# Gate-row offsets and a column copy moved to ScalarE, head selectors made one head ahead, and other reorderings in a hybrid mLSTM/GLA block on Trainium2

## The chip, the cores and the metric

The kernel runs on one core of a Trainium2 chip. The core has a matrix engine (TensorE, PE in the profile), a vector engine (VectorE, DVE), an activation engine (ScalarE, ACT), a general engine (GpSimd, POOL) and SyncE (SP), whose queue issues most DMAs. Each engine runs its own instructions strictly in the order in which the program gave them, and waits by semaphore for what another engine must finish first. The metric is the device time of one execution, in microseconds.

## The reference

One decoder block on 512 positions plus 16 learned meta tokens (padded to 9 chunks of 64), model width 1024, float32. Cut to what matters:

```python
xn = rmsnorm(h, norm1_g)
proj = xn @ w_in                   # split into mq,mk,mv,mi,mf,mo,gq,gk,gv,ga,gr,gate_m,gate_g
mq, mk = split(silu(causal_conv4([mq, mk])))
logi, logf = mi + b_i, log_sigmoid(mf + b_f)            # 4 heads
hm = mlstm_chunkwise(mq * 128**-0.5, mk, mv, logi, logf) # stabilised by a running maximum m_t
hm = head_rmsnorm(hm) * sigmoid(mo)
loga = log_sigmoid(ga @ g_a2 + g_a2_b) / 16
hg = head_rmsnorm(gla_chunked(gq * 128**-0.5, gk, gv, loga)) * silu(gr)
merged = sigmoid(gate_m) * (hm @ w_branch_m) + sigmoid(gate_g) * (hg @ w_branch_g)
h = h + merged @ w_out
ff = silu(hn @ w_ff_gate) * (hn @ w_ff_up)   # hn = rmsnorm(h, norm2_g)
out = rmsnorm(h + ff @ w_ff_down, final_g)
```

Per mLSTM head, position j takes from source s the weight exp(bc_j - bc_s + logi_s - m_j) times q.k; `gate_rows` in the kernel prepares these exponents as rows, and shifts them by each 128-column chunk's distance.

## The kernel before, in words

**Products.** Every weight matrix is streamed as units of 128 x 1024 (tile `raw`, loaded by SP; some parts are added by GpSimd DMAs). A unit is split in two fp32r tiles: ScalarE casts it to `whi` (L190), VectorE takes the difference into `wlo` (L195). Each 128x128 block then costs three matmuls: high by high, high by low, low by high. Plain units run through `mm3` (L304 to L306), 512 or twice 264 columns at a time.

Part of the units come in pairs, done by a Strassen-Winograd scheme: instead of eight half products seven are made, named p7, q1, p3, q6, p4, p2, q5, each four blocks deep and 256 or 272 columns wide (`seven`, L346 to L348). A pair has three PSUM banks: `bx` collects q1, then q6 (with the former p3 pending) and q5; `bz` collects p7 and p4; `by` p2. Between products, banks are copied out while the sum goes on: s1 (ScalarE copy of `bx`) and s7 (of `bz`) when p3 begins, that is, right ahead of q6, which writes on in `bx`; then s2, s5 and others. p3 of a pair is left pending and done in the next pair, at p3's place. Three pairs have no p3 pending when they begin: the first of the merge gates (`gm`, gate_m of the reference), the first of the GLA queries (`gq`) and the first of the feed-forward part. There nothing stands between the first two products and q6. The first merge-gate pair is the first pair of the program.

**Order.** The schedule is written by hand; nothing reorders it. `unit` and `pair` call, after block k of a product, what is due there: the copies of the banks and the split steps for a coming unit (tables `PLAIN`, `FIRST`, `SECOND`, which name the product and block after which each step is issued). Then `tick()` advances the side work by one step: generators that end a step with `yield n`, n being the ticks until the next. `mixers` holds the mLSTM and GLA heads, of which one runs at a time; the others (`side`) run next to each other. So a `yield 6` moves all later steps of that head, and of the heads behind it, six ticks down.

**The steps that the change names.** `gate_rows` builds, on 32 partitions, forget-gate sums `bl`, input exponents `a0` and their running maximum `ml` (whose input `d0` is zeroed first, L658); then ten offset rows (L685), each `bl`'s value at a chunk's end added to 128 columns of a row; TensorE transposes them (L701) into one bank that is copied out as `acol` (L695), and `gts.ready` lets the heads begin. `mlstm` (L877 on) starts a head: a selector (`sel`, cast by ScalarE, L883) picks the head's rows of `gts.R` by two matmuls (L886, L887) into the banks `pb` and `pm`; ScalarE copies `pb` into `nml` (L890), VectorE adds the mask to it (L891), ScalarE takes the exponential of `pm` (`em`). Then come the scores k.q (L908 to L910), the exponentials with `acol` as bias, and their products `wh`, `wl` (L919, L928). Their sum over sources is cast and split (L936, L941) and multiplied with ones (L955). `head_out` normalises a head (L802 to L839), with a Ln, an Exp and so two loads of an activation table. `conv`, `gates_of` and the evacuations of projections (L595, L617) take banks from the same eight. `mixed_x` copies activations for the pairs (L582, L546). `final` (L1487 on) is the last norm.

Of the kernel before, what the change touches and what calls it, by code (L numbers as in the profile page):

```python
# [9 lines left out]
F32R = mybir.dt.float32r  # L10
I32 = mybir.dt.int32
AF = mybir.ActivationFunctionType
ALU = mybir.AluOpType
PSUM = bass.MemoryType.PSUM

P = 128
D = 1024
KT = 8
NM = 16
NS = 512  # L20
NT = NM + NS
HALF = NT // 2
H = 4
DFF = 2816
FT = DFF // P
EPS = 1e-6
TAU = 16.0
QS2 = 128.0
CH = 128
# [73 lines left out]
def hybrid_block(ctx: ExitStack, tc: tile.TileContext, xT, wst, par, con, out):  # L103
# [5 lines left out]
    def nm(s):  # L109
        cnt[0] += 1  # L110
        return f"{s}_{cnt[0]}"
# [6 lines left out]
    def tt(dt=F32, n=NT, p=P):  # L118
        t = tpool.tile([P, TW], dt, tag="t", name=nm("t"))
        return t[:p, :n]  # L120
# [7 lines left out]
    def act(o, i, func, **kw):  # L128
        want = TABLE.get(func)
        if want is not None and table[0] not in want:  # L130
            table[0] = want[0]
            if func != AF.Silu:
                S.preload_act_table_set(want[0])
        S.activation(o, i, func, **kw)  # L134
# [122 lines left out]
    def g_lo(u):  # L257
# [6 lines left out]

    PLAIN = {"s": [(split_hi, 2), (split_lo, 4)], "e": [(e_hi, 1), (e_lo, 3), (s2, 4)],
             "a": [(a_hi, 1), (a_lo, 3), (f_hi, 4), (s4, 5)]}
    FIRST = {"s": [(split_hi, ("q1", 2)), (split_lo, ("p3", 1))],
             "e": [(e_hi, ("q1", 2)), (e_lo, ("p3", 1)), (s2, ("q6", 1))]}
    SECOND = {"s": [(split_hi, ("p2", 0)), (split_lo, ("p2", 2))],
              "a": [(a_hi, ("p2", 0)), (a_lo, ("p2", 2)), (f_hi, ("q5", 0)), (s4, ("q5", 2))],  # L270
              "e": [(e_hi, ("p2", 0)), (e_lo, ("p2", 2)), (s2, ("q5", 2))]}
# [22 lines left out]
    pend = {}  # L294
# [45 lines left out]
    def seven(o, w, x, n, start, hook, c0, c1):  # L340

        wh, wl = w[n]
        xh_, xl_ = x[n]
        for k in range(4):
            h, l = wh[:, k * P:(k + 1) * P], wl[:, k * P:(k + 1) * P]
            T.matmul(o, h, xh_[k][:, c0:c1], start=start and k == 0, stop=False, skip_group_check=not start)  # L346
            T.matmul(o, h, xl_[k][:, c0:c1], start=False, stop=False, skip_group_check=not start)  # L347
            T.matmul(o, l, xh_[k][:, c0:c1], start=False, stop=k == 3, skip_group_check=not start)  # L348
            hook(n, k)

    def pair(names, x, cols, sink):


        u, steps = begin(*names)
        w = mixw[u].w
        bz, bx, by = (bank()[:, :cols[1] - cols[0]] for _ in range(3))
        e = sink(bz, bx, by)
        todo = {("p7", 0): ["s5"], ("p7", 2): ["mid", "c22"], ("q6", 0): ["c12"], ("q6", 2): ["fin"]}
        mine = {("p3", 0): ["s1", "s7"], ("p4", 0): ["s2"], ("p2", 1): ["c21"], ("q5", 0): ["c11"]}
        steps.setdefault(("p7", 3), []).append(lambda: f_lo(u))  # L360
        steps.setdefault(("q6", 1), []).append(lambda: g_hi(u))
        steps.setdefault(("p4", 1), []).append(lambda: g_lo(u))

        def hook(n, k):
            left(*todo.get((n, k), ()))
            for s in mine.get((n, k), ()):
                e.pop(s)()
            for f in steps.get((n, k), ()):
                f()
            if k % 2:  # L370
                tick()

        seven(bz, w, x, "p7", True, hook, *cols)
        seven(bx, w, x, "q1", True, hook, *cols)
        if "p3" in pend:
            pend.pop("p3")(hook)
        else:
            for k in range(4):
                hook("p3", k)
        seven(bx, w, x, "q6", False, hook, *cols)  # L380
        seven(bz, w, x, "p4", False, hook, *cols)
        seven(by, w, x, "p2", True, hook, *cols)
        seven(bx, w, x, "q5", False, hook, *cols)
        assert not pend, pend
        pend.update(e)
        pend["p3"] = lambda hook=lambda n, k: None: seven(bx, mixw.pop(u).w, x, "p3", False, hook, *cols)
# [242 lines left out]
    def gate_rows(ps):  # L629
        a2s = gts.a2s = apool.tile([P, 512], F32R, name="a2s")  # L630
        a2f = pr[:, C_A2:C_A2 + 512]
        gsb = tt()
        for a in range(2):
            c = slice(a * HALF, (a + 1) * HALF)
            V.tensor_tensor(gsb[:96, c], ps[0][a][:96], rstd[:96, c], ALU.mult)
        yield 16
        gam = gts.gam = tt(F32R)
        S.copy(gam[:96], gsb[:96])
        bi = pr[0:32, C_BG:C_BG + 1]
        bf = pr[32:64, C_BG:C_BG + 1]  # L640
        r1, r2, bl, a0 = tt(p=32), tt(p=32), tt(p=32), tt(p=32)
        act(r1, gsb[32:64], AF.Abs, bias=bf)
        yield 1
        act(r1, r1, AF.Exp, scale=-1.0)
        V.tensor_scalar(r2, gsb[32:64], bf, 0.0, op0=ALU.add, op1=ALU.min)
        yield 1
        act(r1, r1, AF.Ln, bias=b_one[:32])
        V.tensor_tensor(gam[64:96], gsb[64:96], gam[64:96].bitcast(F32), ALU.subtract)
        S.copy(a2s[:96], a2f[:96])
        yield 1  # L650
        V.tensor_tensor(r2, r2, r1, ALU.subtract)
        V.tensor_tensor_scan(bl, rmask[:32], r2, 0.0, ALU.mult, ALU.add)
        yield 1
        V.tensor_tensor(a2s[32:64], a2f[32:64], a2s[32:64].bitcast(F32), ALU.subtract)
        V.scalar_tensor_tensor(a0, gsb[0:32], bi, bl, ALU.add, ALU.subtract)
        yield 1
        d0, ml = r1, r2
        V.memset(d0, 0.0)  # L658
        V.tensor_copy(d0[:, CH::CH], bl[:, CH - 1:NT - 1:CH])
        V.tensor_tensor_scan(ml, d0, a0, 0.0, ALU.add, ALU.max)  # L660
        yield 1
        R = gts.R = tt(F32R, NS)
        mr = tt(p=32)
        rhi = d0
        act(R[0:32], ml[:, NM:], AF.Copy, scale=-1.0)
        V.tensor_tensor(mr, ml, bl, ALU.add)
        V.tensor_scalar(mr, mr, -1.0, 40.0, op0=ALU.mult, op1=ALU.min)
        yield 1
        V.scalar_tensor_tensor(R[32:64], ml[:, NM:], -1.0, R[0:32].bitcast(F32), ALU.mult, ALU.subtract)
        S.copy(R[64:96], mr[:, NM:])  # L670
        yield 1
        S.copy(rhi[:, NM:], R[64:96].bitcast(F32))
        yield 1
        V.tensor_tensor(R[96:128], mr[:, NM:], rhi[:, NM:], ALU.subtract)

        acol = gts.acol = apool.tile([P, 480], F32, name="acol")
        gts.idx = {}
        rows = [a0]
        n_ix = 0
        for d in range(NCK):  # L680
            if d > 0:
                nxt = tt(p=32)
                for i in range(NCK - d):
                    e = CH * (i + d) - 1
                    V.tensor_scalar(nxt[:, CH * i:CH * i + CH], rows[-1][:, CH * i:CH * i + CH], bl[:, e:e + 1],  # L685
                                    None, op0=ALU.add)
                rows.append(nxt)
            yield 2
        yield 8
        pst = bank()  # L690
        for d in range(NCK):
            n_ix = gate_cols(pst, rows, d, n_ix)
            yield 1
        yield 2
        V.tensor_copy(acol, pst[:, :480])  # L695
        gts.ready = True

    def gate_cols(pst, rows, d, n_ix):
# [176 lines left out]
    WTOT = off  # L875


    def mlstm(h, q, k, v, gates, dst):
        while not gts.ready or q.v is None or k.v is None:
            yield 1  # L880
        (qh, ql), (kh, kl) = q.v, k.v
        sel = mpool.tile([P, 2, P], F32R, tag="sel", name=nm("sel"))
        S.copy(sel, cn[:, NS + h:NS + 8:H].unsqueeze(2).to_broadcast([P, 2, P]))  # L883
        yield 6
        pb, pm = bank(), bank()
        T.matmul(pb, sel[:, 0], gts.R, start=True, stop=True)  # L886
        T.matmul(pm, sel[:, 1], gts.R, start=True, stop=True)  # L887
        yield 1
        nml, dia, em = tt(n=NS), tt(n=NS), tt(n=NS)
        S.copy(nml, pb)  # L890
        V.tensor_tensor(dia, pb, mask, ALU.add)  # L891
# [595 lines left out]
    def final(a, o):  # L1487
        yield 16
        ps = bank()[:, :HS]
        T.matmul(ps, ones, hsum[a].v, start=True, stop=False)  # L1490
        while o.v is None:
            yield 1
        yield from out_res(7, o.v, a * HS, (a + 1) * HS)
        yield 1
        T.matmul(ps, ones, hsum[a].w, start=False, stop=True)
        yield 1
        y, t = tt(n=HS), tt(n=HS)
        act(y, ps, AF.Ln, bias=b_eps, scale=1.0 / D)
        act(y, y, AF.Exp, scale=-0.5)
        yield 1  # L1500
        V.tensor_tensor(t, y, y, ALU.mult)
        V.scalar_tensor_tensor(t, ps, D * EPS, t, ALU.add, ALU.mult)
        V.tensor_scalar(t, t, -0.5 / D, 1.5, op0=ALU.mult, op1=ALU.add)
        V.tensor_tensor(y, y, t, ALU.mult)
        yield 1
        for j in range(4):
            g = hgain[j, a]
            V.tensor_tensor(g, g, y.unsqueeze(1).to_broadcast([P, 2, HS]), ALU.mult)
            q = S if j % 2 else nc.sync
            q.dma_start(out[2 * j:2 * j + 2, :, a * HS:(a + 1) * HS].rearrange("m p n -> p m n"), g)  # L1510
            yield 1
# [110 lines left out]
```

## Time and profile before

| | before |
|---|---|
| median of 3 runs | 942.75 us (942.73 to 942.78) |
| profiled execution | 943.2 us, span 941.1 us |
| granted TensorE clock, mean | 0.993 |
| PE / DVE / ACT / POOL busy | 98% / 68% / 57% / 9% |
| TensorE matmul instructions | 6083 |
| chain that ended last | PE 88%, DVE 5%, ACT 5% of the span |

The span goes from the first to the last instruction; the profiled execution's own time has 2.1 us around it. Busy shares are for the whole span. Matmuls are pipelined, so that a row's duration is longer than the distance from its start to the next one's. The same holds in part for ScalarE, where consecutive short instructions overlap by about 0.1 us. "Granted clock" is the share of TensorE's full clock that the hardware let through in a stretch.

### The profile page before, as it was taken

To read this page: it belongs to the slowest core of one execution; us is meant where nothing else is said; L and a number is where in the kernel's file an instruction comes from. 1 tells how busy PE (TensorE), PEld (TensorE's weight loads), DVE (VectorE), ACT (ScalarE), POOL (GpSimd) and SP (SyncE) were. 2 spreads that over 40 slices of the span, in tenths; PEclk is the share of its full clock that TensorE was granted. 3 is DMA by queue.
4 is the path that set the end of the run, shared out by engine and by line. 5 is a ranking of instruction groups with operands and counts; after the bars stand their busy time and mean duration, and the time that the engine had idled before them with its cause. 6 is when DMAs were issued, how large, how long until landed. Compare 5 with 4: busy or idle time off the path is not lost.

```text
span 941.1 us, 15476 instructions
## 1 busy us (share of the span) xinstructions
PE 917.7 (98%) x6083; PEld 843.0 (90%) x6083; DVE 641.0 (68%) x948; ACT 536.7 (57%) x947; POOL 86.5 (9%) x102
## 2 busy tenths in 40 slices
PE   6999999989999999999999999999999999999995
PEld 6989999989998899999998888888999999888885
DVE  6898776877865477777777556886767677832323
ACT  7556678779674266767774234443555555732321
POOL 0000022011100011111000000212111210000000
PEclk9999999999999999999999999999999999999998
DMA  6345465355752466565553344244887775332302
GB/s 255 111 132 164 136 141 134 71 125 123 173 143 88 114 152 163 135 139 141 134 137 90 114 141 131 86 124 116 196 187 186 190 179 148 113 108 70 112 1 89
DMA packets 48713, 124.45 MB, mean 132 GB/s; under 512 B 5377, under 2 KB 11521, under 8 KB 48641
## 3 DMA queue, kind: packets, MB, share of 16 engines
q1 hardware_dynamic: 35008, 101.32, 34.6%
q0 software_dynamic: 12544, 21.11, 14.5%
q8 instruction: 47, 0.77, 0.3%
q10 hardware_dynamic: 1088, 1.05, 0.3%
q14 instruction: 26, 0.20, 0.1%
HBM read 118.08 MB, written 5.37 MB: 131 GB/s over the span
## 4 chain that ended last, share of the span: by engine, by line
PE 88%; DVE 5%; ACT 5%; issue 1%; DMA 1%; SPq 0%; DVEq 0%; ACTq 0%
PE b L305 14%; PE b L304 14%; PE b L306 14%; PE b L346 12%; PE b L348 12%; PE b L347 12%; ACT t L134 2%; ACT whi L190 1%; DVE wlo L195 1%; PE b L1069 1%; PE b L1071 1%; PE b L1048 1%; DMA t<-xT 1%; PE b L753 1%; PE b L951 1%
## 5 line engine op out<-in xcount | busy, mean ns | idle before, releaser
L305 PE MATMUL b<-t,whi 128*128 128x512 f32 (+2 forms) x822 | 290.8, 354 | 1.1 <-DVE t L473 0.7
L304 PE MATMUL b<-t,whi 128*128 128x512 f32 (+2 forms) x774 | 274.6, 355 | 6.6 <-ACT t L134 6.6
L306 PE MATMUL b<-t,wlo 128*128 128x512 f32 (+2 forms) x774 | 271.6, 351 | 0.0
L346 PE MATMUL b<-t,whi 128*128 128x256 f32 (+1 forms) x864 | 249.6, 289 | 3.5 <-ACT t L406 2.8
L348 PE MATMUL b<-t,wlo 128*128 128x256 f32 (+1 forms) x864 | 245.3, 284 | 0.0
L347 PE MATMUL b<-t,whi 128*128 128x256 f32 (+1 forms) x864 | 244.5, 283 | 0.0
L195 DVE TENSOR_TENSOR wlo<-raw,whi 128x1024 fp32r<-128x1024 f32 x155 | 193.3, 1250 | 46.2 <-ACT whi L190 45.5
L190 ACT CAST whi<-raw 128x1024 fp32r<-128x1024 f32 x155 | 161.4, 1045 | 62.3 <-PE b L347 26.0
L305 PEld LDWEIGHTS b<-t,whi 128*128 128x128 f32 x822 | 156.4, 190 | 23.7 <-DVE t L473 1.3
L304 PEld LDWEIGHTS b<-t,whi 128*128 128x128 f32 x774 | 147.7, 191 | 26.6 <-ACT t L134 6.6
L346 PEld LDWEIGHTS b<-t,whi 128*128 128x128 f32 x864 | 164.0, 190 | 5.3 <-ACT t L406 3.8
L306 PEld LDWEIGHTS b<-t,wlo 128*128 128x128 f32 x774 | 147.3, 190 | 19.9 <-DVE wlo L195 0.3
L347 PEld LDWEIGHTS b<-t,whi 128*128 128x128 f32 x864 | 163.9, 190 | 0.4
L348 PEld LDWEIGHTS b<-t,wlo 128*128 128x128 f32 x864 | 163.7, 189 | 0.0
L134 ACT ACTIVATE t<-t 128x512 f32<-128x512 f32 (+6 forms) x140 | 80.5, 593 | 58.9 <-DVE t L1098 27.7
L185 POOL DMA_DIRECT2D raw<-wst x36 | 31.1, 864 | 358.2 <-DMA wf<-wst 86.6
L190 ACT CAST whi<-wf 128x1024 fp32r<-128x1024 f32 x36 | 37.8, 1051 | 22.6 <-PE b L347 13.5
L134 ACT ACTIVATE t<-f 128x256 f32<-128x256 f32 (+1 forms) x24 | 11.6, 482 | 61.9 <-DVE f L1469 61.9
L214 POOL DMA_DIRECT2D wf<-wst x36 | 32.1, 901 | 157.2 <-DMA wf<-wst 116.0
L195 DVE TENSOR_TENSOR wlo<-wf,whi 128x1024 fp32r<-128x1024 f32 x36 | 43.8, 1218 | 0.0
L1469 DVE TENSOR_TENSOR f<-f,b 128x512 f32<-128x512 f32 (+1 forms) x9 | 5.6, 628 | 53.6 <-PE b L306 53.6
L346 PE MATMUL b<-t,wgh 128*128 128x256 f32 (+1 forms) x144 | 40.9, 284 | 0.0
(221 smaller groups left out, 1200.6 us busy)
## 6 DMA issues: line engine op xcount, KB each, us to landing
raw<-wst SPq DMA_DIRECT2D x155, 512.0 KB, 3.7
wf<-wst SPq DMA_DIRECT2D x36, 256.0 KB, 3.2
wf<-wst POOLq DMA_DIRECT2D x36, 256.0 KB, 5.6
raw<-wst POOLq DMA_DIRECT2D x36, 256.0 KB, 4.8
t<-xT SPq DMA_DIRECT2D x8, 264.0 KB, 6.1
pos<-t SPq DMA_DIRECT2D x8, 264.0 KB, 2.5
t<-xT SPq DMA_DIRECT2D x8, 256.0 KB, 3.9
t<-neg POOLq DMA_DIRECT2D x6, 272.0 KB, 6.3
```

The costliest lines, as they stand in the source:

```text
L134: S.activation(o, i, func, **kw)
L185: G.dma_start(lr(r, 0), lr(wst[v - 1], 0), accum_op=ALU.add)
L190: S.copy(t, src)
L195: V.tensor_tensor(t, src, hi.bitcast(F32), ALU.subtract)
L214: G.dma_start(lr(st.f, 1), lr(wst[u + 1], 1), accum_op=ALU.add)
L304: T.matmul(o, w_h, ah[:, c0:c1], start=first, stop=False)
L305: T.matmul(o, w_h, al[:, c0:c1], start=False, stop=False)
L306: T.matmul(o, w_l, ah[:, c0:c1], start=False, stop=last)
L346: T.matmul(o, h, xh_[k][:, c0:c1], start=start and k == 0, stop=False, skip_group_check=not start)
L347: T.matmul(o, h, xl_[k][:, c0:c1], start=False, stop=False, skip_group_check=not start)
L348: T.matmul(o, l, xh_[k][:, c0:c1], start=False, stop=k == 3, skip_group_check=not start)
L753: T.transpose(pb[:, c * P:(c + 1) * P], f[:, c * CH:(c + 1) * CH], ident)
```

## The change

1. Ten offset rows (L685) are made by ScalarE (Identity with a bias) and no longer by VectorE; so is the copy `acol` (L695). `d0` becomes a tile of its own, zeroed by GpSimd.
2. The selector of head 0 is cast at the end of the rows' first part, that of head h+1 right after head h's two selector matmuls. There is one buffer for it. The cast in `mlstm` and the `yield 6` behind it go.
3. Pairs with nothing pending begin with q1 and then p7; all others as before.
4. In table `FIRST` the cast of a coming unit is issued at p3's block 0, behind s1 and s7, where it stood at q1's block 2; the difference two blocks later than before, and `s2` one.
5. `final`'s four VectorE steps after Exp become three; the new first one can run beside Ln and Exp.

```diff
-    FIRST = {"s": [(split_hi, ("q1", 2)), (split_lo, ("p3", 1))],
-             "e": [(e_hi, ("q1", 2)), (e_lo, ("p3", 1)), (s2, ("q6", 1))]}
+    FIRST = {"s": [(split_hi, ("p3", 0)), (split_lo, ("p3", 3))],
+             "e": [(e_hi, ("p3", 0)), (e_lo, ("p3", 3)), (s2, ("q6", 2))]}
...
-        seven(bz, w, x, "p7", True, hook, *cols)
-        seven(bx, w, x, "q1", True, hook, *cols)
+        for b, n in ((bz, "p7"), (bx, "q1")) if "p3" in pend else ((bx, "q1"), (bz, "p7")):
+            seven(b, w, x, n, True, hook, *cols)
...
-        d0, ml = r1, r2
-        V.memset(d0, 0.0)
+        d0, ml = tt(p=32), r2
+        G.memset(d0, 0.0)
...
         V.tensor_tensor(R[96:128], mr[:, NM:], rhi[:, NM:], ALU.subtract)
+        selector(0)
...
-                    V.tensor_scalar(nxt[:, CH * i:CH * i + CH], rows[-1][:, CH * i:CH * i + CH], bl[:, e:e + 1],
-                                    None, op0=ALU.add)
+                    act(nxt[:, CH * i:CH * i + CH], rows[-1][:, CH * i:CH * i + CH], AF.Identity,
+                        bias=bl[:, e:e + 1])
...
-        V.tensor_copy(acol, pst[:, :480])
+        S.copy(acol, pst[:, :480])
...
+    def selector(h):
+        gts.sel = mpool.tile([P, 2, P], F32R, tag="sel", name=nm("sel"), bufs=1)
+        S.copy(gts.sel, cn[:, NS + h:NS + 8:H].unsqueeze(2).to_broadcast([P, 2, P]))
+
     def mlstm(h, q, k, v, gates, dst):
...
-        sel = mpool.tile([P, 2, P], F32R, tag="sel", name=nm("sel"))
-        S.copy(sel, cn[:, NS + h:NS + 8:H].unsqueeze(2).to_broadcast([P, 2, P]))
-        yield 6
+        sel = gts.sel
         pb, pm = bank(), bank()
         T.matmul(pb, sel[:, 0], gts.R, start=True, stop=True)
         T.matmul(pm, sel[:, 1], gts.R, start=True, stop=True)
         yield 1
+        del sel
+        if h < H - 1:
+            selector(h + 1)
...
-        y, t = tt(n=HS), tt(n=HS)
+        y, t, x = tt(n=HS), tt(n=HS), tt(n=HS)
         act(y, ps, AF.Ln, bias=b_eps, scale=1.0 / D)
+        V.tensor_scalar(x, ps, D * EPS, -0.5 / D, op0=ALU.add, op1=ALU.mult)
         act(y, y, AF.Exp, scale=-0.5)
         yield 1
         V.tensor_tensor(t, y, y, ALU.mult)
-        V.scalar_tensor_tensor(t, ps, D * EPS, t, ALU.add, ALU.mult)
-        V.tensor_scalar(t, t, -0.5 / D, 1.5, op0=ALU.mult, op1=ALU.add)
-        V.tensor_tensor(y, y, t, ALU.mult)
+        V.tensor_tensor(t, t, x, ALU.mult)
+        V.scalar_tensor_tensor(y, t, 1.5, y, ALU.add, ALU.mult)
```

The lines of the changed kernel stand 1 to 8 lower than those of before from the rows on. What the change does to the order shows at three places.

ScalarE while the gate rows are made, before (L672 is the last copy of `R`'s part; `whi` are weight casts, L513 and the line behind it casts of an input chunk, L757 the cast of head 0's values):

```order
L672 COPY t_486<-t_552 32x512
L190 CAST whi_585<-raw_401 128x1024
L513 CAST t_587<-t_575 128x528
L134 ACTIVATE t_590<-t_575 128x272
L190 CAST whi_645<-raw_476 128x1024
L757 CAST t_647<-b_635 128x512
```

and after, where L759 is that cast of the values (it follows right behind the last row):

```order
L673 COPY t_543<-t_553 32x512
L882 CAST sel_582<-cn 128x256
L190 CAST whi_588<-raw_401 128x1024
L514 CAST t_590<-t_576 128x528
L134 ACTIVATE t_593<-t_576 128x272
L134 ACTIVATE t_600<-t_489,t_488 32x128 x4
L134 ACTIVATE t_613<-t_600,t_488 32x128 x3
L134 ACTIVATE t_624<-t_613,t_488 32x128 x2
L134 ACTIVATE t_643<-t_624,t_488 32x128
L190 CAST whi_648<-raw_476 128x1024
```

The selector and ten rows have come in between; the casts of weights and values stand behind them.

ScalarE just ahead of the first bank copies of the first merge-gate pair, before (L406 and L409 are s1 and s7; `b_2337` and `b_2338` are head 3's selector products):

```order
L134 ACTIVATE t_2320<-b_2140 128x512
L134 ACTIVATE t_2321<-b_2224 128x512
L890 COPY t_2347<-b_2337 128x512
L190 CAST whi_2356<-raw_2141 128x1024
L134 ACTIVATE t_2349<-b_2338,cb 128x512
L406 COPY t_2311<-b_2307 128x256
L409 COPY t_2312<-b_2306 128x256
```

and after (L407 and L410 are s1 and s7; `acol` marks head 3's exponentials, L926 their casts):

```order
L190 CAST whi_2345<-wf_990 128x1024
L926 CAST wh_2197<-t_2302 128x272
L134 ACTIVATE t_2339<-t_2175,acol 128x16
L759 CAST t_2360<-b_2347 128x512
L134 ACTIVATE t_2374<-t_2176,acol 128x16
L926 CAST wh_2197<-t_2339 128x144
L776 CAST t_1801<-b_2380 128x256
L133 ACT_TABLE_LOAD
L134 ACTIVATE t_2401<-b_2214 128x512
L134 ACTIVATE t_2402<-b_2305 128x512
L926 CAST wh_2197<-t_2374 128x16
L407 COPY t_2392<-b_2388 128x256
```

Head 3 is nearly through its exponentials here, where before it had just been started.

TensorE at the start of head 0, before (L304 to L306 are a plain unit of 264 columns at a time; L886 and L887 the selector products):

```order
L304 MATMUL b_858<-t_122,whi_645 128x264
L305 MATMUL b_858<-t_124,whi_645 128x264
L306 MATMUL b_858<-t_122,wlo_664 128x264
L886 MATMUL b_874<-t_552,sel_807 128x512
L887 MATMUL b_875<-t_552,sel_807 128x512
L304 MATMUL b_857<-t_126,whi_645 128x264
```

and after (there L890 and L891):

```order
L304 MATMUL b_769<-t_130,whi_588 128x264
L305 MATMUL b_769<-t_132,whi_588 128x264
L306 MATMUL b_769<-t_130,wlo_608 128x264
L890 MATMUL b_810<-t_553,sel_582 128x512
L891 MATMUL b_811<-t_553,sel_582 128x512
L304 MATMUL b_768<-t_134,whi_588 128x264
```

The two products now stand in the unit before (`whi_588`, which was `whi_585`), 36 weight products earlier.

## The prediction

> **What bounds the kernel now.** I read the busy shares first, then TensorE's waits, then the windows around the two longest of them, then the timeline there.
>
> ```profile
> span 941.1 us, 15476 instructions
> PE 917.7 (98%) x6083; PEld 843.0 (90%) x6083; DVE 641.0 (68%) x948; ACT 536.7 (57%) x947; POOL 86.5 (9%) x102
> ```
>
> TensorE (PE) is busy for 98% of the span. Moving work between the other engines gains time only where TensorE waits for them. Its waits, with total, count and longest:
>
> ```profile
> PE b L346 <- ACT t L406: 2.8, 2, 2.3
> PE b L886 <- ACT sel L883: 2.2, 1, 2.2
> PE b L346 <- ACT t L1391: 0.5, 1, 0.5
> PE b L701 <- DVE t L685: 0.2, 1, 0.2
> ```
>
> The change touches the producers of all four. They come to 5.7 us, but two of them cost more than their idle time. These windows stand around the two long waits; read PE's busy time and PEclk, the granted clock:
>
> ```profile
> 67.89:71.30 3.41, 1.20 (x8) 0.92 (x7) 2.63 (x4) 3.41 (x7) 0.00 (x0) 1.00 0.23 86
> 71.30:74.72 3.42, 3.42 (x17) 3.41 (x16) 3.42 (x8) 0.14 (x1) 0.00 (x0) 0.50 0.60 190
> 207.84:211.25 3.41, 1.39 (x11) 1.39 (x12) 3.41 (x8) 2.23 (x6) 0.86 (x1) 1.00 0.37 56
> 211.25:214.66 3.41, 3.41 (x19) 3.41 (x18) 3.31 (x7) 3.29 (x7) 0.87 (x1) 0.50 0.35 105
> ```
>
> A window in which PE worked 1.20 or 1.39 us is followed each time by 3.4 us at clock 0.50, where half of 3.4 us is lost: 1.7 us. So the selector wait costs 2.2 + 1.7 us and the bank-copy wait 2.3 + 1.7 us.
>
> [...]
>
> **Gate rows and selectors (E1).** Ten offset rows, the column copy and a memset leave VectorE:
>
> ```profile
> L685 DVE TENSOR_SCALAR t<-t,t 32x128 f32<-32x128 f32 x10 | 2.3, 269 | 0.0
> L695 DVE COPY acol<-b 128x480 f32<-128x480 f32 x1 | 0.7, 650 | 0.0
> L658 DVE MEMSET t<- 32x528 f32 x1 | 0.5, 498 | 0.1
> L134 ACT ACTIVATE t<-t,acol 128x128 f32<-128x128 f32 x9 | 3.2, 392 | 0.2 <-PE b L909 0.2
> 56.51 0.31 PE L701 MATMUL b<-pr,t 32*128 32x32 f32 x2
> 57.10 0.58 ACT L757 CAST t<-b 128x512 fp32r<-128x512 f32 x1
> 60.32 0.67 DVE L762 TENSOR_TENSOR t<-b,t 128x512 fp32r<-128x512 f32 x1
> 63.35 1.27 DVE L617 TENSOR_TENSOR t<-b,t 128x512 f32<-128x512 f32 x2
> 64.77 0.60 PE L753 MATMUL b<-pr,t 128*128 128x128 f32 x4
> 66.99 0.41 DVE L595 TENSOR_TENSOR t<-b,t 128x264 f32<-128x264 f32 x1
> 70.30 0.39 ACT L883 CAST sel<-cn 128x256 fp32r<-128x256 f32 x1
> 70.74 0.50 PE L886 MATMUL b<-t,sel 128*128 128x512 f32 x1 [2.21 <-ACT sel L883]
> 75.89 0.56 ACT L890 COPY t<-b 128x512 f32<-128x512 f32 x1
> 78.17 0.67 ACT L134 ACTIVATE t<-b,cb 128x512 f32<-128x512 f32 x1
> ```
>
> VectorE sheds 2.3 + 0.7 + 0.5 = 3.5 us. ScalarE has not run a 32x128 add; the nearest row, 128x128, gives 3.2 / 9, with overlap about 0.3 each, so ten cost 3 us (ends 2 and 4). They queue behind a weight cast and two copies there, so the first four are ready some 0.35 us after TensorE wants them (56.51). The rows now stand ahead of the cast at 57.10, so it ends near 60.3, and VectorE's L762, which follows it, stays where it was at 60.32. Everything behind L762 keeps its time: the gates' copy L617 still starts at 63.35. GpSimd's memset is idle time there; if it were late, VectorE's scan would be late by the 0.5 it sheds.
>
> The selector of head 0 is now cast long before, so its 2.2 us wait goes. But `yield 6` goes too, and the two products stand 36 weight products earlier, 12 ahead of L753 (64.77). At 0.12 us each that is about 63.1. The second one writes the bank that the first L617 reads, 63.35 + 0.67 = 64.0: wait 0.95. The next, head 0's scores, needs the bank of L595, 67.3: 0.5. Two more stand in ScalarE's row: the column copy 0.15, and the exponential of the second selector product (78.17 before). Its bank is wanted 20 products on, and it now comes right behind the next selector and the nml copy (75.89 before): selector's end 70.7 as before, column copy 0.65, nml copy 0.56, exponential 0.67, less 0.3 of overlap, 72.2. PE is there at 68.0 as before, less 0.3, plus 1.4 for selector and score products, plus 1.6 of waits: 70.7. Wait 1.5. Sum 3.45, in five pieces of under 2 us, so I take no half clock. Before: 0.3 + 2.4 (from end to start) + 1.7 = 4.4. E1 = -0.95. Ends: -4.4 if none of the five comes, +0.75 with the half clock again.
>
> **Sum of head 0's weights (E2).** VectorE still carries that head's products to its last one, now 36 products sooner:
>
> ```profile
> 71.88:98.90 27.02, 27.02 (x168) 24.69 (x167) 23.11 (x44) 16.62 (x38) 1.90 (x2) 0.95 0.56 163
> 99.05 0.69 DVE L941 TENSOR_TENSOR t<-t,t 128x512 fp32r<-128x512 f32 x1 [0.69 <-ACT t L936]
> ```
>
> PE no longer gives it the 4 us of the lost wait. It has 23.1 us of work from 72.0, so not before 95.5; with the hand-overs to ScalarE (cast, then difference) I get 99.25. PE has 25 us of products from 72.2 to the low part: 97.2. Wait 0 to 2.05; I take 1.5, nearer the chain, since L941 waited for its cast before too. E2 = +1.5.
>
> **First merge-gate pair (M).** Here the exchange acts (this pair finds nothing pending, so q1 runs first and its bank can be copied 12 products sooner) and so does the earlier start: head 3's exponentials, eight mixing copies and head 2's normalisation, with two activation-table loads, now stand ahead of the bank copies (now L407, L410) in ScalarE's row.
>
> ```profile
> L582 ACT CAST t<-t 128x272 fp32r<-128x272 f32 x8 | 2.8, 424 | 0.3 <-PE b L955 0.3
> L134 ACT ACTIVATE t<-t,acol 128x128 f32<-128x128 f32 x10 | 3.8, 404 | 0.0
> L134 ACT ACTIVATE t<-t,acol 128x16 f32<-128x16 f32 x6 | 1.8, 301 | 0.0
> L134 ACT ACTIVATE t<-t 128x512 f32<-128x512 f32 x4 | 2.5, 625 | 0.0
> L190 ACT CAST whi<-wf 128x1024 fp32r<-128x1024 f32 x2 | 2.1, 1050 | 0.0
> L133 ACT ACT_TABLE_LOAD x1 | 1.3, 1283 | 0.0
> L919 ACT CAST wh<-t 128x400 fp32r<-128x400 f32 x1 | 0.5, 526 | 1.5 <-DVE t L915 1.5
> 190.26 0.40 PE L304 MATMUL b<-t,whi 128*128 128x512 f32 x1
> 190.49 0.40 PE L305 MATMUL b<-t,whi 128*128 128x512 f32 x1
> 192.00 0.28 PE L347 MATMUL b<-t,whi 128*128 128x256 f32 x1
> 192.12 0.28 PE L348 MATMUL b<-t,wlo 128*128 128x256 f32 x1
> 209.86 0.39 PE L346 MATMUL b<-t,whi 128*128 128x256 f32 x1 [2.32 <-ACT t L406]
> ```
>
> The mixing copies reuse the tile that head 2's last product (L818 now) reads, so they cannot start before it. From there to q6, which needs the first bank copy, PE has 30 products of 0.23 (start to start), 24 of 0.12 and 1.3 us of small ones: 11.1 us. ScalarE has in the same stretch, less the 0.1 by which consecutive ones overlap: 8 copies x 0.32, 5 exponentials x 0.3, 4 short ones x 0.2, 5 casts of head 3 at 1.6 together, 5 activations of 512 x 0.52, 2 weight casts x 0.95, 2 table loads x 1.28, 2 small casts 0.8 and the bank copy 0.35: 14.7 us. So PE waits 3.6 us at least, if the stretch starts there. VectorE hands back three of the casts late (L919 waited 1.5 us for it above); followed step by step the bank copy ends 18.8 us after the start: wait 7.7. I take 6.2, nearer the chain, because each link of it has a wait of before as model. One window of 3.4 us then holds too little work, 1.7 more: 7.9. Before, the first two pairs lose 0.3 + 2.5 + 1.7 = 4.5. M = +3.4. Ends: -4.5 (no wait at all) and +6.6 (7.7 and two half-clock windows).
>
> The moved casts of FIRST cost nothing: their products come one pair later, and the copies that they stood ahead of gain.
>
> **Small terms (T).** The bank-copy waits of the other pairs with nothing pending (2.8 - 2.3 = 0.5, and 0.5 at L1391) go, with the 0.1 us hand-over of each: -1.2. The last normalisation:
>
> ```profile
> 933.70 0.43 DVE L1502 SCALAR_TENSOR_TENSOR t<-b,t 128x256 f32<-128x256 f32 x1
> 934.16 0.29 DVE L1503 TENSOR_SCALAR t<-t 128x256 f32<-128x256 f32 x1
> ```
>
> Four dependent steps become three, 934.16 + 0.29 - 0.43 - 933.70 = 0.3 less; the new first step runs beside Ln and Exp. T = -1.5; ends -0.3 and -1.9. SP's mask load moves ahead of one weight load, whose unit comes more than 10 us later: nothing, or that transfer's few us if the cover were gone.
>
> **Sum.** -0.95 + 1.5 + 3.4 - 1.5 = +2.45. The profiled execution took 943.2 us (span 941.1 and 2.1 around it), so it would take 945.65. The median of the runs, 942.75, is 0.45 below it; on that the sum gives 945.2 us.
>
> **Rivals.** *The row before the first pair is hidden (faster).* If ScalarE reaches the mixing copies with time in hand and VectorE, 3.5 us lighter, hands nothing back late (the tile being free sooner than I read from the order), the wait there is about 1 us, under the 2 us that made a half clock: M = -3.5, and E2 is 0. Sum -5.95: 936.8. It decides where that wait passes 2 us. Against it: 14.7 us of work against 11.1. *The waits only move.* M loses as much as the first two pairs did before (0), E2 is 1: -0.95 + 1 - 1.5 = -1.45, 941.3. *More half clock.* The 1.5 us piece and its neighbours fall in one window, and M's wait spans two: 2 x 1.7 on top: 948.6. *The clock dips are not due to these waits.* Then both dips of before stay, and the 6.2 us wait adds its own: +0.75 + 1.5 + 5.1 - 1.5 = +5.85, 948.6. [...]
>
> **How the numbers follow.** Forecast 0.45 (943 to 948), hidden row 0.25, moved waits 0.20, more half clock 0.06, dips not due to waits 0.04. A change of 0.2%, 1.9 us, is about what a measurement here can tell from none: faster is below 940.9, slower above 944.6. Faster: 0.25 and 0.04 of the moved waits, 0.29. Slower: 0.35 of the forecast and 0.10, 0.45. Same: the rest, 0.26. The range takes the upper end of the hidden row and the half-clock cases: 937.5 to 949.
>
> **What would show it.** Right: TensorE's wait list has no selector entry but entries of 1 to 2 us for gate copies and an exponential between 60 and 75 us; a wait of 5 us or more on the first bank copy near 205 us, and a 0.50 window behind it; about 1.5 us for the low part of head 0's sum near 97 us; nothing at 333 and 650 us. Wrong: that bank-copy wait is under 2 us, or the clock stays at 1.00 after a wait of over 3 us.

## The result, and the profile after

The changed kernel takes 949.44 us (median of 4 runs: 947.75, 948.1, 950.78, 950.96) against 942.76 for the one before: ratio 1.0069, 95% interval 1.0047 to 1.0092. It is slower, as forecast, but by 6.7 us and not by 2.4, and just outside the range. The profiled execution took 948.1 us, span 946.3, which is 5.2 us over the span before.

Rows of TensorE's waits in the changed kernel (engine, line, what it waited for; total, count, longest); three that the kernel before has too are left out:

```profile
PE b L304 <- ACT t L134: 8.2, 2, 6.6
PE b L346 <- ACT t L407: 5.5, 1, 5.5
PE b L346 <- ACT t L408: 2.2, 1, 2.2
PE b L348 <- DVE wlo L195: 1.0, 3, 0.4
PE b L891 <- DVE t L618: 0.6, 1, 0.6
PE b L963 <- DVE t L948: 0.6, 1, 0.6
PE b L346 <- DVE t L922: 0.3, 1, 0.3
PE b L915 <- DVE t L596: 0.2, 1, 0.2
```

All four waits that the change was aimed at are gone from the list. What came in: the second part of the first line (8.2 - 6.6 = 1.6 us, the exponential of the second selector product), the gates' copy (L618), head 0's scores (L596), head 0's sum (L963), and at the first merge-gate pair 5.5 us on s1 (L407). One long entry was in no step of the prediction: 2.2 us on s2 (L408).

The windows at the first pair, and then at that second place (length, busy time of PE, PEld, DVE, ACT and POOL, granted clock, DMA share, GB/s):

```profile
196.65:200.06 3.41, 1.12 (x10) 0.92 (x8) 2.85 (x7) 0.94 (x4) 0.00 (x0) 1.00 0.46 141
200.06:203.47 3.41, 0.21 (x1) 0.21 (x2) 2.34 (x7) 3.38 (x9) 0.86 (x1) 0.50 0.16 33
203.47:206.89 3.42, 3.42 (x17) 3.42 (x18) 2.43 (x4) 2.37 (x5) 0.23 (x1) 0.50 0.56 136
234.19:237.60 3.41, 1.75 (x14) 1.53 (x13) 3.34 (x6) 3.38 (x6) 0.17 (x1) 1.00 0.97 149
237.60:241.02 3.42, 2.92 (x23) 2.92 (x24) 3.42 (x7) 2.24 (x7) 0.00 (x0) 1.00 0.35 134
```

The half clock lasts two windows here, but TensorE works only 0.21 us of the first and 3.42 us of the second, and half of that is lost: 1.8 us. ScalarE's row ahead of s1, from the timeline (start, duration, what; x n are consecutive ones; in brackets idle time and who ended it):

```profile
184.97 1.39 ACT L583 CAST t<-t 128x272 fp32r<-128x272 f32 x4 [1.70 <-PE b L818]
...
189.27 1.28 ACT L133 ACT_TABLE_LOAD   x1
...
196.09 0.42 ACT L926 CAST wh<-t 128x272 fp32r<-128x272 f32 x1 [0.60 <-DVE t L922]
...
199.86 0.31 ACT L926 CAST wh<-t 128x144 fp32r<-128x144 f32 x1 [2.47 <-DVE t L922]
...
200.47 1.28 ACT L133 ACT_TABLE_LOAD   x1
201.76 1.09 ACT L134 ACTIVATE t<-b 128x512 f32<-128x512 f32 x2
...
202.82 0.39 ACT L407 COPY t<-b 128x256 f32<-128x256 f32 x1
```

The mixing copies wait 1.7 us for head 2's last product, as read from the order; from there to s1's end it takes 18.2 us (the step-by-step chain said 18.8), of which 3.1 are handed back late by VectorE. And TensorE, which needs that copy, had its last product before it at 197.5.

### The profile page after: what moved, and what is told of

It reads as the page before. It is cut to its first block, busy times and chain, and to the rows that moved or that the text cites. A ratio compares the mean times of both kernels' runs of the same rounds, so it can differ in the third digit from the quotient of the medians.

```text
span 946.3 us, 15470 instructions
## 1 busy us (share of the span) xinstructions
PE 917.1 (97%) x6083; PEld 841.4 (89%) x6083; DVE 637.7 (67%) x936; ACT 537.3 (57%) x957; POOL 87.3 (9%) x103
## 4 chain that ended last, share of the span: by engine, by line
PE 86%; DVE 6%; ACT 5%; issue 1%; DMA 1%; SPq 0%; DVEq 0%; ACTq 0%
PE b L304 14%; PE b L305 14%; PE b L306 14%; PE b L346 12%; PE b L348 12%; PE b L347 12%; ACT t L134 2%; ACT whi L190 1%; DVE wlo L195 1%; PE b L1076 1%; PE b L1078 1%; PE b L1055 1%; ACT L133 1%; PE b L958 1%; DMA t<-xT 1%
## 5 line engine op out<-in xcount | busy, mean ns | idle before, releaser
L304 PE MATMUL b<-t,whi 128*128 128x512 f32 (+2 forms) x774 | 274.0, 354 | 8.2 <-ACT t L134 8.2
L306 PE MATMUL b<-t,wlo 128*128 128x512 f32 (+2 forms) x774 | 270.6, 350 | 0.0
L304 PEld LDWEIGHTS b<-t,whi 128*128 128x128 f32 x774 | 146.7, 189 | 28.2 <-ACT t L134 8.4
L306 PEld LDWEIGHTS b<-t,wlo 128*128 128x128 f32 x774 | 146.4, 189 | 20.2 <-DVE wlo L195 0.4
L134 ACT ACTIVATE t<-t 128x512 f32<-128x512 f32 (+5 forms) x140 | 80.4, 594 | 59.3 <-DVE t L1105 27.7
L214 POOL DMA_DIRECT2D wf<-wst x36 | 34.1, 955 | 153.7 <-DMA wf<-wst 93.4
L1398 ACT COPY t<-b 128x256 f32<-128x256 f32 x48 | 16.4, 375 | 43.6 <-PE b L348 43.6
```

Of the source, the lines that this page charges most:

```text
L214: G.dma_start(lr(st.f, 1), lr(wst[u + 1], 1), accum_op=ALU.add)
L304: T.matmul(o, w_h, ah[:, c0:c1], start=first, stop=False)
L306: T.matmul(o, w_l, ah[:, c0:c1], start=False, stop=last)
L1398: s7=lambda: S.copy(s[:, lo], bz), s1=lambda: S.copy(s[:, hi], bx), s2=lambda: S.copy(r[:, lo], bx),
```

## The experiments

**The six ticks put back.** The heads then start as late as before, but for the selector that is ready; all other parts are as changed.

```diff
         sel = gts.sel
+        yield 6
         pb, pm = bank(), bank()
```

> The changed kernel with the pause of six ticks put back between taking the selector and its two matmuls; everything else as changed. Theory A (the heads' earlier start fills ScalarE's row ahead of the bank copies of the first pairs): the 5.5 us wait on L407 near 200 us, the 2.2 us wait on L408 near 236 us and the half-clock stretch go, the selector wait of before stays away: 934 to 940 us. Rival B (the rows and the column copy on ScalarE are the load that delays its row): the waits stay above 3 us in sum, 945 us or more. Rival C (the exchange of q1 and p7): unchanged too, 946 to 950 us.

939.16 us, ratio 0.997 (0.996 to 0.9979). Three of TensorE's waits in it:

```profile
PE b L346 <- ACT t L408: 2.0, 1, 2.0
PE b L892 <- ACT acol L697: 1.4, 1, 1.4
PE b L346 <- ACT t L407: 1.4, 1, 1.4
```

10 us of the changed kernel's time hang on this one line, and with it the change is a gain of 0.3%. Both long waits are gone from their places, at the first pair and near 236 us. The waits of 1.4 us on s1 and 2.0 us on s2 stand at the second pair, at 207.5 and 214.5 us, where the kernel before waited 2.3 us on s1. Theory A is borne out in both long waits and in the time, but not in the half clock: a window of it follows this wait on s2 (shown below). Rivals B and C, which had 945 us or more, are out.

**The selectors alone** on the kernel before, with the ticks dropped:

```diff
-        sel = mpool.tile([P, 2, P], F32R, tag="sel", name=nm("sel"))
-        S.copy(sel, cn[:, NS + h:NS + 8:H].unsqueeze(2).to_broadcast([P, 2, P]))
-        yield 6
+        sel = gts.sel
```

> The kernel before with the change's selectors alone: head 0's cast behind the rows' first part, head h+1's behind head h's matmuls, the six ticks dropped. Theory A: as slow as the changed kernel or slower by the small gains that it lacks, 947 to 952 us, with a wait of 4 to 6 us on the first bank copy of the first pair. Rivals B and C: the selector wait of 2.2 us and its half clock go and nothing comes in their place, 938 to 941 us.

949.42 us, ratio 1.0078 (1.0064 to 1.0092), with 6.1 us on the first pair's copy:

```profile
PE b L346 <- ACT t L406: 7.6, 3, 6.1
PE b L346 <- ACT t L407: 1.2, 1, 1.2
```

This one part makes the whole loss; what the other four parts win together is about nothing once it is there. At the third pair it has two waits, 1.0 us on s1 at 232 us and 1.2 on s2 at 238, where the changed kernel has one of 2.2 us on s2.

**Rows and column copy back on VectorE**, else as changed:

```diff
-                    act(nxt[:, CH * i:CH * i + CH], ..., AF.Identity, bias=bl[:, e:e + 1])
+                    V.tensor_scalar(nxt[:, CH * i:CH * i + CH], ..., bl[:, e:e + 1], None, op0=ALU.add)
...
-        S.copy(acol, pst[:, :480])
+        V.tensor_copy(acol, pst[:, :480])
```

> The changed kernel with the ten offset rows and the column copy back on VectorE. Theory A: the long waits near 200 and 236 us stay, since the rows lie 140 us ahead of them; only the waits between 60 and 75 us change, by under 2 us: 947 to 951 us. Rival B: 943 us or less.

947.9 us, ratio 1.006 (1.0047 to 1.0072): the long waits stay (5.2 and 2.1 us), so rival B is out. Its early waits came to 3.0 us from start to start, against 3.7 in the changed kernel (profile of each): moving the rows did not help where it was made. The difference of the two times is inside their intervals.

**p7 ahead of q1 everywhere**, else as changed:

```diff
-        for b, n in ((bz, "p7"), (bx, "q1")) if "p3" in pend else ((bx, "q1"), (bz, "p7")):
+        for b, n in ((bz, "p7"), (bx, "q1")):
```

> The changed kernel with p7 ahead of q1 in every pair, as before. Theory A: the copy s1 is late because of what stands ahead of it in ScalarE's row and not because of its bank, so the long wait stays within 0.5 us of 5.5; the short waits of 0.5 us at the other pairs with nothing pending may come back: 948 to 952 us. Rival C (the exchange brings the loss): 944 us or less.

950.35 us, ratio 1.0082 (1.0068 to 1.0095), so rival C is out again: 5.4 us on L407 still, and 0.5 on L407 and on L1398 at the two later pairs with nothing pending. At the first pair 1.1 and 5.6 us stand for the 0.5, 0.5 and 5.65. So the exchange wins half a microsecond at each later pair with nothing pending and nothing at the first, by the rows; the two times are inside each other's intervals.

**The exchange and the later casts alone** on the kernel before:

> The kernel before with two parts of the change alone: q1 ahead of p7 in pairs with nothing pending, and the later casts of table FIRST. Theory A (these parts gain, the heads' earlier start loses): the cast of 1.0 us no longer stands ahead of s1 at 207 us, so that wait falls from 2.3 to about 1.3 us, under what a half clock followed so far, and the waits at 333 and 650 us go: -1.0 - 1.7 - 1.2, some 939 us, with the selector wait and its half clock still there. Rival (the copy at 207 us is late for another reason, head 3's products on VectorE): the wait stays over 2 us, only 1.2 us are won, 941.5 us.

941.12 us, ratio 0.9988 (0.9979 to 0.9996), nearer to the rival. The wait at 207 us fell to 1.4 us as theory A has it, but a new one of 2.0 us on s2 stands 7 us behind. ScalarE's rows there say why; first the kernel before:

```profile
209.46 0.35 ACT L406 COPY t<-b 128x256 f32<-128x256 f32 x1
...
211.34 0.42 ACT L919 CAST wh<-t 128x272 fp32r<-128x272 f32 x1 [1.27 <-DVE t L915]
...
215.53 0.36 ACT L407 COPY t<-b 128x256 f32<-128x256 f32 x1
```

and with the exchange and the casts:

```profile
208.21 0.35 ACT L406 COPY t<-b 128x256 f32<-128x256 f32 x1
...
211.04 0.42 ACT L919 CAST wh<-t 128x272 fp32r<-128x272 f32 x1 [1.26 <-DVE t L915]
...
215.24 0.36 ACT L407 COPY t<-b 128x256 f32<-128x256 f32 x1
```

The copy of s1 (L406) comes 1.25 us earlier, since the weight cast now runs behind it. But ScalarE then waits for VectorE's hand-back (L915) until 211.04, 0.3 earlier than before, and a table load and two activations follow, so the copy of s2 (L407) is 0.3 us earlier only. TensorE comes earlier by what it saved at s1 and waits at s2 instead: the wait is handed on.

**A pause ahead of the last head only:**

```diff
         sel = gts.sel
+        if h == H - 1:
+            yield 24
         pb, pm = bank(), bank()
```

> The changed kernel with a pause of 24 ticks ahead of the last head's selector matmuls, so that heads 0 to 2 start as early as changed and head 3 about where it did before. Theory A, as now read: what fills ScalarE's row ahead of the first pair's bank copies are head 3's exponentials on top of head 2's normalisation; with head 3 behind them the 5.5 us wait falls under 2 us and the 2.2 us one near 236 us goes; the early waits (2.9 us) and that for head 0's sum (0.8 us) stay: 936 to 941 us. Rival D (the early start of all heads, not the last one's, brings the loss): 946 us or more.

937.75 us, ratio 0.9953 (0.9941 to 0.9966). Rows of its waits:

```profile
PE b L304 <- ACT t L134: 8.2, 2, 6.6
PE b L346 <- ACT t L407: 1.1, 2, 0.7
PE b L965 <- DVE t L950: 0.5, 1, 0.5
```

The 5.5 us wait and the 2.2 us one are gone together, with heads 0 to 2 as early as in the changed kernel. Both belong to the place of head 3 and of the GLA heads, which run behind it and are put off with it. Rival D is out. The early waits stay, as expected.

**Half that pause** (12 ticks):

> The changed kernel with a pause of 12 ticks, not 24, ahead of the last head's selector matmuls. Theory A: about half of head 3's row still stands ahead of the first bank copy; a wait of 1 to 4 us on L407 near 200 us, 940 to 946 us. If the whole loss hangs on one collision that 12 ticks already undo: 938 us.

942.66 us, ratio 1.0002 (0.9993 to 1.0011): s1 waits 1.0 us only, but

```profile
PE b L346 <- ACT t L408: 2.4, 1, 2.4
PE b L346 <- ACT t L407: 1.2, 2, 1.0
```

s2 waits 2.4 us near 230 us, and behind a window with 1.21 us of TensorE's work a half-clock window follows (230.39 to 233.81, clock 0.50). So the two waits are two collisions: twelve ticks undo the first and leave the second.

**What stands ahead of s2.** In the changed kernel, ScalarE near 236 us:

```profile
231.27 1.06 ACT L190 CAST whi<-raw 128x1024 fp32r<-128x1024 f32 x1
232.22 1.70 ACT L134 ACTIVATE t<-t 128x512 f32<-128x512 f32 x3
233.80 0.73 ACT L134 ACTIVATE t<-t,cb 128x528 f32<-128x528 f32 x1
...
235.33 1.28 ACT L133 ACT_TABLE_LOAD   x1
236.63 1.15 ACT L134 ACTIVATE t<-t 128x512 f32<-128x512 f32 x2
237.68 0.37 ACT L408 COPY t<-b 128x272 f32<-128x272 f32 x1
```

Head 3's normalisation and the first GLA head's decay are there side by side, then a table load and the merge gates' activations (`fin` of the pair before). The test moves `fin` behind s2:

```diff
-        todo = {..., ("q6", 2): ["fin"]}
+        todo = {..., ("p4", 1): ["fin"]}
```

> The changed kernel with one step of every pair moved: the closing activations of the pair before (fin, with their table load) stand behind the bank copy s2 and no longer ahead of it. Theory A for the wait on L408 near 236 us: the table load (1.3) and two activations (1.1) ahead of s2 make it late; it falls from 2.2 to under 0.4 us, and with it the half clock that followed in some runs: 944.5 to 947 us, the 5.5 us wait unchanged. Rival: s2 is late because of head 3's normalisation and the decay's exponentials before them; then over 1.5 us stay and the time is 948 us or more.

950.71 us, ratio 1.0089 (1.0075 to 1.0103): neither way. The wait on L408 is gone, and 2 to 4 us later this has come:

```profile
PE b L348 <- DVE wlo L195: 2.1, 3, 1.6
PE b L346 <- ACT whi L190: 1.0, 1, 1.0
```

The weight cast now stands behind `fin`. What makes the wait, as I read it, is the sum of ScalarE's work in that stretch and not the order of two steps; reordering these two steps only moves it: 1.0 and 1.6 us now, 2.2 and 0.4 us before. No other pair has a new wait of over 0.3 us. The profiled span is 2.5 us longer than the changed kernel's all the same, and two half-clock windows stand behind these waits (up to 248.06):

```profile
237.82:241.24 3.42, 1.69 (x12) 1.25 (x10) 3.42 (x7) 2.26 (x7) 0.00 (x0) 1.00 0.28 111
241.24:244.65 3.41, 2.55 (x11) 2.55 (x12) 3.29 (x5) 1.83 (x5) 0.00 (x0) 0.50 0.12 22
```

**TensorE kept busy through most of the long wait,** with 40 products into the pair's third bank, which the pair itself begins later:

```diff
+            if names[0] == ("gm", 0):
+                for i in range(40):
+                    T.matmul(by, w["q1"][0][:, :P], x["q1"][0][0][:, cols[0]:cols[1]], start=True, stop=True)
         seven(bx, w, x, "q6", False, hook, *cols)
```

> The changed kernel with 40 products more (4.7 us) on TensorE, written to the first pair's third bank, which is only begun later, at the place of the 5.5 us wait; they change no result. If the half clock follows from TensorE's idle windows: the wait on L407 is about 1 us, the clock near 200 us stays at 1.00 and about 1.8 us are won, 945.5 to 947 us in the profile's run where the changed kernel's had 948.1. If the half clock has another cause, it stays at 0.50 for 6.8 us near 200 us and the time is 948 to 951 us.

947.76 us (947.66 to 948.43 in 5 runs), ratio 1.0058 (1.0045 to 1.0072), 948.25 in the profiled run, above the 945.5 to 947 expected. The median is 1.7 us under the changed kernel's, the size that was forecast (1.8), but inside the intervals. The products began 1.5 us into the wait, since VectorE was not done with what the bank held before, and no wait on s1 was left:

```profile
PE b L383 <- DVE t L767: 1.5, 1, 1.5
```

The clock at the place stayed at 1.00:

```profile
196.95:200.36 3.41, 1.87 (x16) 1.66 (x15) 2.93 (x7) 0.94 (x4) 0.00 (x0) 1.00 0.38 115
200.36:203.77 3.41, 3.41 (x32) 3.41 (x32) 2.34 (x7) 3.38 (x9) 0.86 (x1) 1.00 0.15 46
```

With TensorE idle for 1.5 us and no longer for 5.5, and 1.87 us of work in the window instead of 1.12, there is no half clock at this place: it was the idle time that brought it there. From ahead of the wait to the last product ahead of 236 us the profiled run gains 1.1 us on the changed kernel's (0.4 us behind, then 0.7 us ahead). There it loses 1.5 us again: the wait near 236 us, the same to 0.1 us (2.2 us), was followed by a half-clock window this time and in the changed kernel's profile was not.

**When a wait is followed by a half clock.** Windows around waits of 2.0 to 2.2 us, in three of these kernels; the first row of each holds the wait. The six ticks put back:

```profile
211.10:214.51 3.41, 1.47 (x13) 1.27 (x11) 2.32 (x7) 3.38 (x8) 0.87 (x1) 1.00 0.22 73
214.51:217.93 3.42, 3.39 (x15) 3.39 (x16) 3.14 (x10) 2.96 (x5) 0.00 (x0) 0.50 0.71 161
```

the exchange and casts alone:

```profile
211.95:215.37 3.42, 1.71 (x15) 1.50 (x13) 2.32 (x7) 3.39 (x7) 0.87 (x1) 1.00 0.29 37
215.37:218.78 3.41, 3.13 (x25) 3.13 (x26) 3.13 (x9) 3.00 (x6) 0.00 (x0) 1.00 0.83 204
```

rows back on VectorE:

```profile
235.50:238.91 3.41, 1.27 (x10) 1.05 (x9) 3.38 (x5) 2.88 (x8) 0.00 (x0) 1.00 0.76 199
238.91:242.32 3.41, 3.41 (x17) 3.41 (x17) 3.41 (x8) 2.76 (x5) 0.00 (x0) 0.50 0.04 14
```

In the profile of the kernel before the clock changes at 71.30, 74.72, 211.25 and 214.66 us, in that of the changed kernel at 200.06 and 206.89. Within a profile these lie whole multiples of 3.413 us apart (139.95 us, 41 times that, from 71.30 to 211.25), and the windows of a profile are taken along its changes. Counted back from the first change (20 and 58 windows), they begin at 3.04 us in the one profile and at 2.09 us in the other, so a wait falls on them as it may. Of the windows at full clock shown here, those with 1.12, 1.20, 1.21, 1.27, 1.39, 1.47 and 1.69 us of TensorE's work were followed by half the clock, and those with 1.71, 1.75 and 1.87 us were not. The profiles of before and of the changed kernel have no other window at full clock with less than 2 us of work between 14 us and the last norm. The three waits above lie on both sides: with the ticks back and with the rows back a single window holds 1.94 and 2.14 us of idle time (3.41 less 1.47 and less 1.27), and half of the next 3.4 us, 1.7 us, was lost; with the exchange and casts alone one window holds 1.71 us of it and the next 0.28 us, and the clock stayed at 1.00.

The changed kernel's wait near 236 us is of this kind (1.75 in its window, above). Its four runs stand in two groups, 947.8 to 948.1 us at a mean clock of 0.993 to 0.995 and 950.8 to 951.0 us at 0.990. Whether this wait makes the upper group was not seen, as only a run of the lower group was profiled. One half-clock window took 1.7 us (half of 3.41) and the groups lie 2.7 us or more apart, so it would need about two, as the profiled run with `fin` behind s2 has them there (950.61 us, mean clock 0.990).

Ahead of the last norm, the half-clock stretches lasted 3.41 and 3.42 us in the kernel before and 6.83 us in the changed one (200.06 to 206.89). The windows at full clock ahead of half-clock ones were in no case shown here idle as a whole: TensorE worked 1.12 to 1.69 us in them.

**The column copy on VectorE, with the six ticks back.**

> The changed kernel with the six ticks put back, as in the first experiment (939.2), and the column copy back on VectorE. There TensorE waited 1.4 us for the bank that ScalarE copies out at L697. If that is ScalarE's row, VectorE, without the ten rows, copies in time: -1 to -1.6 us, 937.6 to 938.2. If VectorE's row is as late there (it copied at 69.3 us before, and the selector came at 70.7): no change beyond 0.5 us.

939.62 us, ratio 0.9973 (0.9963 to 0.9983): no change. The wait is 1.4 us as before, now for VectorE's copy, and the next one (L764) grew from 0.7 to 1.1 us. Both engines' rows are equally late there.

**em ahead of the nml copy,** and in a second kernel the rows and column copy back on VectorE as well, both with the last head's pause of 24:

```diff
-        if h < H - 1:
-            selector(h + 1)
         nml, dia, em = tt(n=NS), tt(n=NS), tt(n=NS)
+        act(em, pm, AF.Exp, bias=b_lnq)
         S.copy(nml, pb)
...
         yield 1
-        act(em, pm, AF.Exp, bias=b_lnq)
+        if h < H - 1:
+            selector(h + 1)
         yield 1
```

> The kernel with the last head's pause of 24 ticks (937.75), and in every head the exponential of the second selector product ahead of the nml copy and of the next selector's cast in ScalarE's row. TensorE waited 1.6 us for its bank near 71 us. Theory A (ScalarE's row is the limit there, in its order): 0.8 us less, the copy and the cast no longer ahead; 936.6 to 937.1 us. If the wait passes to the bank of the nml copy: no change, 937.5 to 938.

> The same as the run before it, and the ten offset rows and the column copy back on VectorE. From the third experiment, where the waits up to 98 us came to 3.0 us and not 3.7: 0.5 to 0.8 us less than the run before it, 936 us or a little above. If ScalarE's lighter row matters less once the exponential stands first, or VectorE's sum of head 0 gets later: within 0.3 us of the run before it.

938.81 us, ratio 0.9961 (0.9949 to 0.9973), and 937.28 us, ratio 0.9945 (0.9931 to 0.9958). Neither is as expected: the first is 1.1 us above the pause alone, where 0.8 us less or no change was expected, and the second 1.5 us under the first, where 0.5 to 0.8 was; the intervals overlap both times. In the first, the wait for em fell, from 8.2 - 6.6 = 1.6 us to 0.9, and the one for head 0's sum took it over:

```profile
PE b L304 <- ACT t L134: 7.5, 2, 6.6
PE b L965 <- DVE t L950: 1.6, 1, 1.6
```

The second went from 0.5 to 1.6 us. VectorE's part of that sum (L950) begins at 97.2 us with em ahead and in the kernel with the pause alone, so TensorE only waits sooner or later for it. VectorE's row isn't full, though. With em ahead:

```profile
94.88 0.69 DVE L764 TENSOR_TENSOR t<-b,t 128x512 fp32r<-128x512 f32 x1 [2.02 <-ACT t L759]
...
97.23 0.69 DVE L950 TENSOR_TENSOR t<-t,t 128x512 fp32r<-128x512 f32 x1
```

VectorE stands idle for 2.0 us ahead of L764, for a cast that is behind a weight cast in ScalarE's row. And with the rows back on VectorE (the second kernel), L950 comes 0.8 us sooner and not later. So VectorE's work alone does not set its time; the hand-overs between the two engines have a part in it. The second kernel has the lowest median of the study, 0.55% under the one before, though not clear of the 937.75 of the pause alone.

## Why the prediction was wrong, step by step

Direction and main mechanism held, the sum did not. Its terms against the two profiles (from start to start on TensorE):

| term | predicted | measured | |
|---|---|---|---|
| E1, gate rows and selectors | -0.95 | -1.5 | waits of 0.7, 0.4 and 1.75 us for 3.45 in all; no half clock |
| E2, head 0's sum | +1.5 | +0.8 | between the ends, nearer the lower |
| M, first merge-gate pair | +3.4 | +4.2 | 0.5, 0.5 and 5.65 us, 0.3 and the half clock's 1.8, less 4.5 before |
| T, later pairs and last norm | -1.5 | -1.35 | 0.7 + 0.7 gone, 0.4 new at 347 us, 0.34 at the end |
| the pair near 236 us | none | +3.2 | 2.3, 0.6 and 0.3 us |
| sum | +2.45 | +5.35 | spans differ by 5.2 |

The table counts waits and half clock only; smaller differences, such as first products that already ran 0.7 us sooner, are not in it and about cancel. The four terms that were forecast come to +2.15 for +2.45 with errors of 0.15 to 0.8 us that offset one another, which is luck. The profiled executions differ by 4.9 us (948.1 for 943.2) and the medians by 6.7: 1.3 us of the rest are due to the upper group of runs (949.44 lies between 948.1 and 950.78), whose cause no profile shows. The lower group lies within the range.

**The step that failed is a term that the sum put at nothing without a reason: the pairs behind the first two.** The paragraph on the small terms lets later pairs only win: "The bank-copy waits of the other pairs with nothing pending (2.8 - 2.3 = 0.5, and 0.5 at L1391) go". I followed head 3's earlier steps to the first pair and stopped there. The same earlier start brings its normalisation to the GLA head's decay, two pairs on, and makes s2 late: 3.2 us there, more than the whole forecast. The experiment with a pause ahead of the last head shows it, since it removes this wait along with the first, and the one with half the pause shows it apart. The order of ScalarE's row told of it as plainly as of the first collision: a table load, six activations and a 1.06 us weight cast between the copies s7 and s2.

**E1** held in kind: the selector's wait went and three smaller ones came, one each on the gates' copy, the scores' bank and the exponential; only the column copy's and the first rows' did not show as waits (0.2 us or less). That VectorE gains nothing from shedding the rows was right: the experiment with them back was no slower.

**E2** was mis-sized, 0.8 for 1.5. TensorE came for head 0's sum when forecast (97.0 for 97.2 us), but VectorE's part was ready at 97.8. The forecast had 99.25 by the chain worked out by hand and 95.5 by VectorE's work alone: if its work took what was summed, the hand-overs cost 2.3 us, not 3.75. The largest is the 2.0 us at L764, as above.

**M** was the likeliest case and its working holds: the mixing copies were held by the reused tile, ScalarE's own work is 15.2 us of the 18.2 (14.7 forecast), and the two hand-backs from VectorE are the 0.6 and the 2.5 us above. I took 6.2 us between 3.6 and 7.7; it was 6.6 with the two small waits. Both table loads are in that stretch, but they are not both head 2's: its Ln and its Exp follow the one at 189.27 with no load between them, and the one at 200.47 stands ahead of two activations out of banks.

**The moved casts** were said to cost nothing. They were not run apart from the exchange, but two runs bear on it. Where the two stand alone, the gain at s1 that was booked in full is taken back by s2 (2.0 us, new): between s1 and s2 ScalarE is held by VectorE's hand-back and its own row, which did not move. And at the third pair, near 236 us, the weight cast that stood ahead of s1 now stands between s7 and s2. With the selectors alone that pair waits 1.0 + 1.2 us, in the changed kernel 2.2 us in one piece: the same sum, but a half clock followed the single wait in the profiled runs with the rows back (2.1 us, 1.27 us of work in its window), with p7 first (2.1 us, mean clock 0.991 for the changed kernel's 0.993) and with the 40 products (2.2 us), while with the selectors alone the mean clock is the changed kernel's 0.993.

**The rivals.** The hidden row was refuted by 5.5 us, and the waits that only move by M's +4.2. That the dips are not due to these waits is refuted by the 40 products, and by the kernel with the pause of 24 ticks, whose longest wait from 14 us to the last norm is 1.6 us and whose clock is never halved in between (mean 0.997). "More half clock" (0.06) came true in part: two half-clock windows follow the first pair's wait, but cost 1.8 us and not 3.4, since TensorE worked 0.21 us of the first. I priced the half clock as a thing of a kernel; with waits of 2.0 to 2.2 us it came in some profiled runs and not in others, and for a median it should have been a chance at each such wait.

## What to carry to other kernels

A pause in a hand-written order that looks idle can be what keeps two chains apart: before taking it out, follow everything behind it to the end of the chain, not to the first place where it meets the bottleneck engine. Where one part of a bundle moves many later steps, run it alone and run the rest without it: here one line of a five-part change turned a gain of 0.3% into a loss of 0.7%, and put ahead of the last head alone a longer pause gave 0.5%. When a wait is taken away and the next one grows by as much, the time is set elsewhere: look for what the other engine is waiting for in that stretch before calling it full.

## What the runs showed of the hardware that was not expected

A wait's cost depended on where it fell against the clock's changes, which lie whole multiples of 3.413 us apart within a profile. Windows at full clock with 1.12, 1.20, 1.21, 1.27, 1.39, 1.47 and 1.69 us of TensorE's work were followed by half the clock, those with 1.71, 1.75 and 1.87 us were not. So the same wait of 2.2 us near 236 us was followed by half the clock in one profiled run (with the 40 products) and not in another (the changed kernel's). That this makes the two groups of the changed kernel's runs, some 3 us apart, is not shown.

Windows at half clock with 0.21 us (changed kernel) and 2.55 us of work (`fin` behind s2) were followed by another one at half clock; those with 3.41 and 3.42 us (before and changed kernel) were followed by the full clock.

Products that no one needs, put into the 5.5 us wait from 1.5 us on, kept the clock at 1.00 in both windows there (1.87 and 3.41 us of work).
